# Six or eight column tiles side by side in a decoder layer's first products, in place of four

## The chip, the cores and the metric

The kernel runs on one core of one Trainium2 chip. The metric is the device time of one execution in microseconds; the number given is the median of several executions. All times below are microseconds unless marked ns.

## The reference

One step of a decoder layer on 264 tokens (256 of a prompt, 8 single-token samples), model width 2048:

```
h += 1/2 * RMSNorm_post(SwiGLU_1(RMSNorm_pre(h)))       feed-forward 1, inner width 5632
u  = RMSNorm_pre(h); proj = u @ w_in                    2048 -> 10288 columns:
     conv group (a, b) 2x1024 | z 3072 | xBC 5120 | dt 48
  conv group: GLU -> 31-tap causal convolution -> LayerNorm -> swish
  state-space group: 4-tap causal convolution -> SiLU -> chunked scan
                     (48 heads in 8 groups, state 128) -> RMSNorm gated with SiLU(z)
h += RMSNorm_post(concat(conv 1024, ssm 3072) @ w_out)
h += 1/2 * RMSNorm_post(SwiGLU_2(RMSNorm_pre(h)))       feed-forward 2
h += RMSNorm_post(sigmoid(RMSNorm_pre(h) @ w_gate) * (p @ w_proj))   per-layer embedding
```

Everything is float32, and the states and the sample rows of the convolutions are outputs too.

## The kernel before, in words

Activations lie transposed: features on the 128 partitions, the 264 tokens along a row. A matrix of K rows and M columns is cut into 128x128 weight tiles, K/128 row tiles by M/128 column tiles. The product for one column tile is accumulated in one PSUM bank over all row tiles.

**Three products for one.** A float32 product is made of float32r parts. The input tile is split into a rounded part and the rest (`split`, L248 to L257: ACT rounds, DVE subtracts); so is the weight tile (L151: ACT rounds `whi`; L152: DVE subtracts and leaves `wlo`). `mm3` (L242) issues three matmuls for each pair of tiles, at L244, L245 and L246.

**The weights' stream.** `Weights` (L125) walks a list of units, `_plan` (L70), each at most 16 weight tiles. A unit is loaded in halves of up to 8 tiles (512 KB) by SP, each half rounded by ACT and subtracted by DVE. There are four buffers of 8 tiles for the raw, the rounded and the rest part; two units are asked for ahead of the one in use (`AHEAD`). A buffer comes free when the matmuls that read its tiles are done.

**Two loops over the weights.** `gemm_one` (L342) makes one column tile from one unit of 16 rows: it needs all 16 input tiles. `gemm_first` (L330) is used where a stage's input tiles are only being made: its units hold 4 rows by 4 column tiles, and four banks are accumulated side by side, so that each new input tile is followed by 4 x 3 matmuls. It is called in feed-forward 1 and 2 (L371), in the input projection (L786), in the output projection (L852) and in the per-layer embedding (L928).

**PSUM.** Eight banks: a pool of five for column tiles (`acc_tile`, L184) and a pool of three for everything else (`ps_tile`, L187): the sums of squares, transposes, the state-space part.

**Who reads the banks.**
- Feed-forward: `mid` (L363) takes a gate bank and an up bank: DVE multiplies the gate by the scale `r` (L365), ACT applies SiLU, DVE multiplies by the up bank (L368). `r` comes from the sum of squares over all input tiles (`sq.total()`, L296) through Ln and Exp on ACT.
- Input projection: the order of the column tiles is fixed in `_in_order` (L43): dt, then for each of eight groups B, C, x, (b and a of the conv group in groups 1, 2, 4 and 6), x, x, z, z, z. So the first ten are dt, B, C, x0, x1, x2, z0, z1, z2, B of group 1. `do_dt` (L548) reads its bank once (L551) and then computes time steps and decays, with a round trip through DRAM (L569 to L576) before ACT's Exp at L577. `do_conv` (L598) reads its bank with two ACT instructions (L600, L601) and three of DVE (L603). A z bank is read by one SiLU (L812).
- Per-layer embedding: the bank is read once, times `r` (L939).

**What sets the order.** Instructions are traced in program order, and a scheduler lays them on the engines at compile time by priority (program order; the weights ahead of the rest) and by its own estimate of when each can run. Each engine then works through its list in that fixed order. ACT functions that need a table (SiLU; Ln and Exp) are held in program order by `table` and `act` (L228 to L240), so that a SiLU traced after `do_dt` runs after `do_dt`'s Exp.

Of the kernel before, what the change touches and what calls it, by code (L numbers as in the profile page):

```python
# [21 lines left out]
NS = 8  # L22
# [15 lines left out]

GLU_IN = (1, 2, 4, 6)


# ---------------------------------------------------------------- layout plan
def _in_order():  # L43
    """Column tiles of the input projection in the order they are computed."""
# [25 lines left out]
def _plan():  # L70
    """Weight units in order of use: (matrix, row tiles, column tiles), row tile slowest."""
# [3 lines left out]
    def ffn(i):  # L75
        gu = f"gu{i}"
        for q in range(4):
            plan.append((gu, k16[4 * q : 4 * q + 4], [0, 1, 2, 3]))
        for lo, hi in FF_CHUNKS:
            for f in range(max(lo, 2), hi):  # L80
                plan.append((gu, k16, [2 * f]))
                plan.append((gu, k16, [2 * f + 1]))
            for m in range(KD):
                plan.append((f"dn{i}", list(range(lo, hi)), [m]))
# [4 lines left out]
    first = [m for _, m in IN_ORDER[:4]]  # L89
    for q in range(4):  # L90
        plan.append(("in", k16[4 * q : 4 * q + 4], first))
    for _, m in IN_ORDER[4:]:
        plan.append(("in", k16, [m]))
# [8 lines left out]
    for q in range(4):  # L102
        plan.append(("pg", k16[4 * q : 4 * q + 4], [0, 1, 2, 3]))
    for m in range(4, KD):
        plan.append(("pg", k16, [m]))
# [5 lines left out]
# columns of the small-parameter block  # L111
# [13 lines left out]
class Weights:  # L125
    """Streams the weight units: load, round to float32r, keep what rounding left."""
# [8 lines left out]
    def load(self, between=()):  # L135
        """The next unit, in halves; runs a function of `between` ahead of each half."""
# [29 lines left out]
def kernel(ctx: ExitStack, tc: tile.TileContext, a: dict):  # L166
# [10 lines left out]
    # ------------------------------------------------------------ helpers  # L177
# [50 lines left out]
    def table(name):  # L228
        """Functions that need a table run in program order, so that tables change only here."""
# [18 lines left out]
    def split(x, gain=None):  # L248
        """float32r halves of x (times a gain per partition)."""
# [9 lines left out]
    class SumSq:  # L259
        """Sum of squares over tiles and partitions, on every partition. The last `direct` tiles  # L260
        go to the tensor engine by themselves."""
# [19 lines left out]
        def add_plain(self, s):  # L281
            """Adds the tile s itself."""
# [16 lines left out]
    def rsqrt(out, x, bias=0.0, scale=1.0):  # L299
        """(scale * x + bias) ** -0.5"""  # L300
# [3 lines left out]
    def rms_scale(p, n):  # L304
        """1 / sqrt(p / n + eps)"""
        r = rtile()
        rsqrt(r, p, eps1, 1.0 / n)
        return r

    # ------------------------------------------------------------ constants  # L310
# [10 lines left out]
    # ------------------------------------------------------------ residual stream  # L321
# [5 lines left out]
    bg = deque()  # work that fills in between the matrix products  # L327

    # ------------------------------------------------------------ feed-forward
    def gemm_first(xs, kts, nunits):  # L330
        accs = [acc_tile() for _ in range(4)]
        n = 0
        total = nunits * 4
        for _ in range(nunits):
            w = ws.next()
            for kk in range(4):
                for m in range(4):
                    mm3(accs[m], w[4 * kk + m], xs[kts[n]], n == 0, n == total - 1)
# [13 lines left out]
    def ffn(xs, sq, done):  # L352
        """xs: split gained input; sq: its sum of squares. Calls done(m, y) on each finished
        column tile y (without the input scale); returns eps * (mean square + eps) of the input."""
# [16 lines left out]
        accs = gemm_first(xs, k16, 4)  # L371
        mid(0, accs[0], accs[1])
        mid(1, accs[2], accs[3])
        ys = [None] * KD
        for c, (lo, hi) in enumerate(FF_CHUNKS):
            for f in range(max(lo, 2), hi):
# [20 lines left out]
    def ffn_scale(p, eq):  # L397
        """1 / 2 / sqrt(mean(y^2) + eps / scale^2): the post-norm of scale * y, halved, where
        eq = eps / scale^2."""
# [13 lines left out]
    # ============================================================ FFN 1  # L413
# [8 lines left out]
    for q in range(4):  # L422
        ws.load([lambda k=4 * q + i: load_x(k) for i in (0, 2)])
# [5 lines left out]
    # sample conv history: sums over the saved rows  # L429
# [33 lines left out]
    # y for the post-norm; h . y and y . y (with the gain) for the next pre-norm  # L463
# [22 lines left out]
    # mean square of h + rs y, from the parts  # L486
# [8 lines left out]
    # per-layer embedding projection: independent of the residual stream  # L495
# [13 lines left out]
    # u = rmsnorm(h + rs y), two tiles behind the update of h  # L509
# [15 lines left out]
    # ============================================================ mixer  # L525
# [3 lines left out]
    # causal triangle: row token s, column token l, l >= s  # L529
# [6 lines left out]
    tm = mp.tile([P, 2, 2, NH], F32, name="tm")          # token-major dt, dt*A per chunk  # L536
    acs = mp.tile([P, 2, NH], F32, name="acs")           # token-major cumulative sums
    dte = mp.tile([P, 2, NH], F32, name="dte")           # decay to the end of the chunk
    cd = mp.tile([P, NH], F32, name="cd")                # decay over chunk 1
    dtp = mp.tile([P, 24, NS], F32, name="dtp")          # sample dt on (head, p)  # L540
    eap = cpool.tile([P, 24, NS], F32, name="eap")       # sample decay on (head, p)
# [543 lines left out]
```

## Time and profile before

| | |
|---|---|
| median of 3 executions | 2482.04 (2472.21 to 2486.53) |
| span of the profiled execution, which is all the profile gives of its time | 2479.2 |
| granted TensorE clock, mean | 0.990 |
| matmuls at L244, L245, L246 | 6320 each |
| weight halves of 512 KB, of 256 KB | 774, 32 |
| wait of ACT's weight rounding (L151) on matmuls to free a buffer | 733.5 |
| input tiles made in feed-forward 1 / input projection / feed-forward 2 / embedding, from about | 7 / 796 / 1566 / 2355 |

How to read the views. The table of windows cuts the span into stretches; for each it gives the length, then for each engine the busy time and in brackets the number of instructions, then the granted clock of TensorE (1.00 is full), the share of the DMA engines and GB/s. A busy TensorE can still be slow: matmuls overlap in their records, so their number in a stretch says more than the busy time. The list of waits says which engine waited at which line for which, with the total, the number of times and the longest. A row of the timeline is start, duration, engine, line, operation, output and inputs, and in square brackets the idle time just before with what ended it.

### The profile page before, as it was taken

How to read it: one execution, taken by the hardware profiler on the slowest of the kernel's cores; microseconds unless marked ns; L12 is line 12 of the kernel's file. 1: busy time of each engine (PE TensorE's matmuls, PEld its weight loads, DVE VectorE, ACT ScalarE, POOL GpSimd, SP SyncE). 2: the span in 40 equal slices, each digit the busy share in tenths (PEclk: the TensorE clock that was granted, in tenths of full speed). 3: DMA queues.
4: the chain of work that ended last, by engine and by line, in shares of the span. 5: the costliest groups of instructions: out<-in, count | busy, mean ns of one | idle time of the engine just before them, and what ended most of it. 6: DMA issues, size and time to landing. Idle time of an engine off the chain costs nothing.

```text
span 2479.2 us, 47214 instructions
## 1 busy us (share of the span) xinstructions
PE 2405.7 (97%) x19432; PEld 2380.9 (96%) x19432; DVE 1593.6 (64%) x2249; ACT 1179.2 (48%) x1761; POOL 348.6 (14%) x329
## 2 busy tenths in 40 slices
PE   8999999999999999999999999899999999999996
PEld 8999999999999889999998999899999999999996
DVE  6554455545557858979898965855545655555585
ACT  6444444433456465555655454544444443344463
POOL 2500000000015212121112011410000000000142
PEclk9999999999999999999999999999999999999998
DMA  7655555555556665666665547467666776675653
GB/s 242 211 181 180 180 179 179 180 180 181 181 167 214 200 199 191 214 208 197 210 212 187 180 162 231 140 232 235 221 211 221 237 236 206 210 239 191 193 171 114
DMA packets 160201, 489.88 MB, mean 198 GB/s; under 512 B 23360, under 2 KB 40304, under 8 KB 159984
## 3 DMA queue, kind: packets, MB, share of 16 engines
q1 hardware_dynamic: 159984, 486.85, 60.9%
q8 instruction: 152, 2.49, 0.4%
q14 instruction: 65, 0.53, 0.1%
HBM read 465.65 MB, written 22.42 MB: 197 GB/s over the span
## 4 chain that ended last, share of the span: by engine, by line
PE 86%; DVE 7%; DMA 2%; ACT 2%; issue 2%; POOL 1%; SPq 0%; DVEq 0%; ACTq 0%; POOLq 0%
PE acc L244 28%; PE acc L246 28%; PE acc L245 28%; DVE wlo L152 2%; DVE y L213 1%; DVE h L210 1%; DVE tmp L213 1%; ACT whi L151 1%; DVE act L213 1%; PE ps L729 1%; PE ps L296 0%; POOL run L210 0%; DMA ab<-d_cs 0%; PE ps L714 0%; DMA wraw<-in_w 0%
## 5 line engine op out<-in xcount | busy, mean ns | idle before, releaser
L244 PE MATMUL acc<-act,whi 128*128 128x264 f32 x6320 | 1801.0, 288 | 16.8 <-ACT whi L151 8.4
L245 PE MATMUL acc<-act,whi 128*128 128x264 f32 x6320 | 1804.2, 286 | 12.5 <-DVE act L213 6.3
L246 PE MATMUL acc<-act,wlo 128*128 128x264 f32 x6320 | 1802.4, 286 | 3.6 <-DVE wlo L152 3.6
L152 DVE TENSOR_TENSOR wlo<-wraw,whi 128x1024 fp32r<-128x1024 f32 (+1 forms) x806 | 992.3, 1233 | 612.7 <-ACT whi L151 610.0
L151 ACT CAST whi<-wraw 128x1024 fp32r<-128x1024 f32 (+1 forms) x806 | 828.1, 1031 | 994.7 <-PE acc L245 733.5
L245 PEld LDWEIGHTS acc<-act,whi 128*128 128x128 f32 x6320 | 1203.6, 190 | 17.9 <-DVE act L213 8.6
L246 PEld LDWEIGHTS acc<-act,wlo 128*128 128x128 f32 x6320 | 1199.1, 190 | 7.7 <-DVE wlo L152 5.2
L244 PEld LDWEIGHTS acc<-act,whi 128*128 128x128 f32 x6320 | 1186.6, 189 | 19.9 <-ACT whi L151 8.4
L210 POOL TENSOR_TENSOR run<-run,tmp 128x264 f32<-128x264 f32 x135 | 129.8, 962 | 982.3 <-ACT tmp L237 978.8
L210 POOL TENSOR_TENSOR s<-s,eap 128x1024 f32<-128x1024 f32 x24 | 47.3, 1972 | 608.2 <-DMA s<-in_hst 586.4
L213 DVE SCALAR_TENSOR_TENSOR y<-v,vec,y 128x247 f32<-128x247 f32 (+23 forms) x240 | 124.5, 540 | 1.1
L213 DVE SCALAR_TENSOR_TENSOR s<-bb,xds,s 128x128 f32<-128x128 f32 x192 | 52.6, 347 | 62.9 <-POOL s L210 62.9
L210 POOL TENSOR_TENSOR h<-h,cbc 128x1024 f32<-128x1024 f32 x24 | 65.4, 2738 | 165.3 <-DVE y L213 72.1
L210 DVE TENSOR_TENSOR tmp<-acc,rr 128x264 f32<-128x264 f32 x104 | 44.7, 431 | 64.0 <-PE acc L246 63.9
L252 ACT CAST act<-tmp 128x264 fp32r<-128x264 f32 x120 | 48.6, 409 | 62.3 <-DVE tmp L210 47.5
L210 DVE TENSOR_TENSOR tmp<-tmp,acc 128x264 f32<-128x264 f32 x88 | 37.6, 427 | 45.6 <-PE acc L246 44.8
L210 DVE TENSOR_TENSOR act<-tmp,act 128x264 fp32r<-128x264 f32 x120 | 54.3, 457 | 0.0
L210 DVE TENSOR_TENSOR y<-y,acc 128x264 f32<-128x264 f32 x80 | 34.0, 425 | 26.5 <-PE acc L246 26.5
L237 ACT ACTIVATE tmp<-tmp 128x264 f32<-128x264 f32 x112 | 46.8, 418 | 8.3 <-DVE tmp L210 8.0
L237 ACT ACTIVATE tmp<-y 128x264 f32<-128x264 f32 x67 | 28.1, 426 | 42.3 <-DVE y L210 41.2
L213 DVE SCALAR_TENSOR_TENSOR act<-h,vec,act 128x264 fp32r<-128x264 f32 x48 | 35.2, 756 | 6.4 <-ACT act L237 6.4
L237 ACT ACTIVATE act<-h,vec 128x264 fp32r<-128x264 f32 x48 | 23.8, 512 | 31.3 <-POOL h L210 15.2
(148 smaller groups left out, 800.7 us busy)
## 6 DMA issues: line engine op xcount, KB each, us to landing
wraw<-in_w SPq DMA_DIRECT2D x774, 512.0 KB, 4.7
h<-in_hst SPq DMA_DIRECT2D x24, 512.0 KB, 4.9
s<-in_hst SPq DMA_DIRECT2D x24, 512.0 KB, 6.4
out_nss<-s SPq DMA_DIRECT2D x24, 512.0 KB, 2.8
wraw<-in_w SPq DMA_DIRECT2D x32, 256.0 KB, 3.7
ab<-d_cs SPq DMA_DIRECT2D x16, 384.0 KB, 4.2
cbc<-d_bc SPq DMA_DIRECT2D x8, 512.0 KB, 4.2
bb<-d_bc SPq DMA_DIRECT2D x8, 512.0 KB, 7.4
```

The source lines that it names most:

```text
L151: nc.scalar.copy(hi, raw)
L152: nc.vector.tensor_tensor(out=lo, in0=raw, in1=hi.bitcast(F32), op=ALU.subtract)
L210: return (eng or nc.vector).tensor_tensor(out=out, in0=in0, in1=in1, op=op)
L213: return nc.vector.scalar_tensor_tensor(out=out, in0=in0, scalar=scalar, in1=in1, op0=op0, op1=op1)
L237: i = nc.scalar.activation(out=out, in_=in_, func=func, bias=bias, scale=scale)
L244: nc.tensor.matmul(acc, hi, x[:, 0, :], start=first, stop=False)
L245: nc.tensor.matmul(acc, hi, x[:, 1, :], start=False, stop=False)
L246: nc.tensor.matmul(acc, lo, x[:, 0, :], start=False, stop=last)
L252: nc.scalar.copy(t[:, 0, :], x)
L729: nc.tensor.matmul(pd[64 * q : 64 * q + 64, P * c : P * c + P], xdt[c][:, 2 * j + q, :], ab[c][:, 2 * j + q, :], start=True, stop=True,)
```

## The change

`gemm_first` gets the number of columns as an argument. In feed-forward 1 and 2 and in the per-layer embedding it is 6, in the input projection 8; in the output projection it stays 4. Banks beyond five come from the pool of three: one with 6 columns, three with 8. They are the first ones: the first gate tile, the first embedding tile, and dt, B and C. Units for these calls hold 2 rows by 6 or 8 columns (12 tiles, loaded as 8 and 4; or 16), eight units instead of four. The columns that move into the wide group leave the list of single columns. The loads of feed-forward 1's first units are written out in eight steps of two input tiles and one unit, where they were four steps of two input tiles, half a unit, two input tiles, half a unit. All arithmetic and all weight bytes are the same.

```diff
+FIRST_FF, FIRST_IN, FIRST_PG = 6, 8, 6
...
     def ffn(i):
         gu = f"gu{i}"
-        for q in range(4):
-            plan.append((gu, k16[4 * q : 4 * q + 4], [0, 1, 2, 3]))
+        for q in range(8):
+            plan.append((gu, k16[2 * q : 2 * q + 2], list(range(FIRST_FF))))
         for lo, hi in FF_CHUNKS:
-            for f in range(max(lo, 2), hi):
+            for f in range(max(lo, FIRST_FF // 2), hi):
...
-    first = [m for _, m in IN_ORDER[:4]]
-    for q in range(4):
-        plan.append(("in", k16[4 * q : 4 * q + 4], first))
-    for _, m in IN_ORDER[4:]:
+    first = [m for _, m in IN_ORDER[:FIRST_IN]]
+    for q in range(8):
+        plan.append(("in", k16[2 * q : 2 * q + 2], first))
+    for _, m in IN_ORDER[FIRST_IN:]:
...
-    for q in range(4):
-        plan.append(("pg", k16[4 * q : 4 * q + 4], [0, 1, 2, 3]))
-    for m in range(4, KD):
+    for q in range(8):
+        plan.append(("pg", k16[2 * q : 2 * q + 2], list(range(FIRST_PG))))
+    for m in range(FIRST_PG, KD):
...
-    def gemm_first(xs, kts, nunits):
-        accs = [acc_tile() for _ in range(4)]
+    def gemm_first(xs, kts, nunits, nm=4):
+        accs = [ps_tile([P, T]) if m < nm - 5 else acc_tile() for m in range(nm)]
         n = 0
-        total = nunits * 4
+        per = len(kts) // nunits
         for _ in range(nunits):
             w = ws.next()
-            for kk in range(4):
-                for m in range(4):
-                    mm3(accs[m], w[4 * kk + m], xs[kts[n]], n == 0, n == total - 1)
+            for kk in range(per):
+                for m in range(nm):
+                    mm3(accs[m], w[nm * kk + m], xs[kts[n]], n == 0, n == len(kts) - 1)
                 n += 1
...
-        accs = gemm_first(xs, k16, 4)
-        mid(0, accs[0], accs[1])
-        mid(1, accs[2], accs[3])
+        accs = gemm_first(xs, k16, 8, FIRST_FF)
+        for f in range(FIRST_FF // 2):
+            mid(f, accs[2 * f], accs[2 * f + 1])
...
-    for q in range(4):
-        ws.load([lambda k=4 * q + i: load_x(k) for i in (0, 2)])
+    for q in range(8):
+        ws.load([lambda k=2 * q: load_x(k)])
...
-    first = gemm_first(us, k16, 4)
+    first = gemm_first(us, k16, 8, FIRST_IN)
...
-        acc = first[n] if n < 4 else gemm_one(us, k16)
+        acc = first[n] if n < FIRST_IN else gemm_one(us, k16)
...
-    accs = gemm_first(xs, k16, 4)
+    accs = gemm_first(xs, k16, 8, FIRST_PG)
...
-        acc = accs[m] if m < 4 else gemm_one(xs, k16)
+        acc = accs[m] if m < FIRST_PG else gemm_one(xs, k16)
```

More of the change, by code (lines that the diff above doesn't have):

```diff
@@ L369, in mid @@
             mids[f] = split(p)
-        accs = gemm_first(xs, k16, 4)
-        mid(0, accs[0], accs[1])
-        mid(1, accs[2], accs[3])
+        accs = gemm_first(xs, k16, 8, FIRST_FF)
+        for f in range(FIRST_FF // 2):
+            mid(f, accs[2 * f], accs[2 * f + 1])
         ys = [None] * KD
         for c, (lo, hi) in enumerate(FF_CHUNKS):
-            for f in range(max(lo, 2), hi):
+            for f in range(max(lo, FIRST_FF // 2), hi):
                 pg = gemm_one(xs, k16)
```

## The prediction, made before the changed kernel was run

> **What bounds the kernel now.** I read the page's busy times first, then the table of windows over the stages that call `gemm_first`, then TensorE's waits in those stages, then the timeline at their ends.
>
> ```profile
> span 2479.2 us, 47214 instructions
> PE 2405.7 (97%) x19432; PEld 2380.9 (96%) x19432; DVE 1593.6 (64%) x2249; ACT 1179.2 (48%) x1761; POOL 348.6 (14%) x329
> 310.00:372.00 62.00, 62.00 (x510) 62.00 (x509) 31.80 (x37) 25.33 (x32) 0.00 (x0) 1.00 0.56 179
> ```
>
> TensorE bounds the kernel as a whole. The third row is an undisturbed stretch of feed-forward 1: 510 matmuls in 62 us, 0.1216 us each at the full clock. One column tile of 16 rows is 48 matmuls, 5.83 us; one input tile against four columns is 12 (1.46), against six 18 (2.19), against eight 24 (2.92). The number of these matmuls does not change, so only lost TensorE time can be won.
>
> ```profile
> 802.60:838.60 36.00, 29.43 (x205) 28.06 (x204) 33.38 (x47) 15.64 (x27) 17.45 (x19) 0.91 0.71 235
> 838.60:872.50 33.90, 33.90 (x275) 33.27 (x274) 22.07 (x39) 15.35 (x28) 0.00 (x0) 1.00 0.55 150
> 1568.20:1605.00 36.80, 33.53 (x240) 32.34 (x241) 35.10 (x47) 22.31 (x44) 20.61 (x21) 0.92 0.34 106
> 2357.00:2394.00 37.00, 33.76 (x243) 32.58 (x244) 34.85 (x48) 22.67 (x44) 21.31 (x21) 0.93 0.44 140
> ...
> PE acc L246 <- DVE wlo L152: 1.1, 1, 1.1
> PE ps L296 <- POOL run L210: 0.5, 1, 0.5
> ...
> PE acc L245 <- DVE act L210: 6.0, 4, 1.9
> PE acc L244 <- ACT act L252: 0.5, 1, 0.5
> ...
> PE acc L245 <- DVE act L213: 3.1, 4, 1.1
> ```
>
> Columns of the windows: PE, PEld, DVE, ACT, POOL, clock, DMA. The first row is the input projection's first columns, the third feed-forward 2's, the fourth the embedding's. DVE works 33.4 of 36.0, 35.1 of 36.8 and 34.9 of 37.0: it makes the input tiles and the weights' rest parts, and TensorE waits for it. The waits are those inside the stages: feed-forward 1 (two rows, 1.6 in all), input projection (6.0 + 0.5), feed-forward 2 (3.1; the embedding's answer has the same row). In the input projection 205 matmuls take 24.9 at the full clock, so 11.1 of 36.0 is lost: 6.5 waited, 3.2 to the clock (36.0 x 0.09), the rest to slower pairs. So the change can win at most 1.6 + 11.1 + 3.1 + 3.1 = 18.9, 0.8% of the span.
>
> **The change part by part.** *Balance per input tile.* What DVE spends on weights, and on all else, in the time that the tiles are made:
>
> ```profile
> 1566.40:1602.00 35.60, 19.74 (x70) 14.31 (x70) 10.75 (x8) 0.90 0.33 106
> 802.60:833.00 30.40, 14.93 (x52) 11.35 (x52) 10.71 (x7) 0.89 0.72 238
> L152 DVE TENSOR_TENSOR wlo<-wraw,whi 128x512 fp32r<-128x512 f32 x32 | 22.1, 690 | 0.6
> ```
>
> The first two rows count only instructions that touch `wlo` (third bracket: DVE). Seven subtractions of 8 tiles (the eighth of the first row only begins there) take 10.7, 0.19 per weight tile; the rest of the stretch, 24.9 and 19.7, makes 16 input tiles, 1.55 and 1.23 each. Feed-forward 2: four columns cost DVE 1.55 + 0.76 = 2.31 per tile against TensorE's 1.46; six cost 2.70 against 2.19. DVE stays the slower one, but buffers filled ahead cover some of it. Input projection: 1.23 + 0.76 = 1.99 against 1.46; with eight 2.75 against 2.92. There TensorE becomes the bound, which is why this term is the largest. The units of 12 need a subtraction of 4 tiles each, 690 ns: 0.17 per tile, so the cut costs DVE nothing; twelve more SP issues, casts and subtractions in all are hidden behind DVE's own list.
>
> *The new wait.* With four columns one of the five banks is free when the group ends, so the next column starts at once. With six or eight the pool of five is full: the next `gemm_one` waits until DVE has read a bank, and behind its first matmul on TensorE's list stand all later ones. ACT and DVE are not held and refill two units of weights meanwhile. Also, the waits inside the group can no longer be filled with the next column's matmuls.
>
> ```profile
> 1600.59 1.39 DVE L213 SCALAR_TENSOR_TENSOR act<-h,vec,act 128x264 fp32r<-128x264 f32 x2
> 1605.39 0.43 DVE L210 TENSOR_TENSOR tmp<-tmp,acc 128x264 f32<-128x264 f32 x1 [0.88 <-ACT tmp L237]
> 2389.24 1.40 DVE L213 SCALAR_TENSOR_TENSOR act<-h,vec,act 128x264 fp32r<-128x264 f32 x2
> 2392.68 0.77 DVE L210 TENSOR_TENSOR tmp<-acc,rr 128x264 f32<-128x264 f32 x2 [0.92 <-PE acc L246]
> 1568.26 1.25 PE L244 MATMUL acc<-act,whi 128*128 128x264 f32 x4 [2.94 <-ACT act L237]
> 2357.02 1.25 PE L244 MATMUL acc<-act,whi 128*128 128x264 f32 x4 [3.41 <-ACT act L237]
> ```
>
> *Feed-forward 2.* The last input tile is done at 1602.0. Two units of 12 are ready beforehand, so 72 weight tiles remain, 13.7, and the last tile moves to 1566.4 + 24.9 + 13.7 = 1605.0; TensorE ends 2.19 later, 1607.2. It has then had 1607.2 - 1568.3 = 38.9 for 288 matmuls, 35.0, and 2.9 of half clock (36.8 x 0.08): 1.0 of waits is left, so 2.1 of 3.1 is won. The first bank of the five (the up tile of pair 0) now comes free 3.8 after the last input tile (1602.0 to 1605.8: total, Ln, Exp, gate times `r`, SiLU, times up): 1608.8, a wait of 1.6. Net -0.5.
>
> *Embedding.* The same, but bank two is read only once, 2.8 after the last tile (2390.6 to 2393.4). Wait 2.8 - 2.2 = 0.6; won 2.1 less that, net -1.5.
>
> *Feed-forward 1.* Here TensorE sets the pace already and `r` is known long before the end. Two rows now bring 768 KB of weights and 270 KB of x, and at the rate of this row
>
> ```profile
> 12.00:16.00 4.00, 4.00 (x28) 4.00 (x28) 4.00 (x5) 4.00 (x9) 3.60 (x3) 1.00 1.05 398
> ...
> L237 ACT ACTIVATE tmp<-tmp 128x264 f32<-128x264 f32 x112 | 46.8, 418 | 8.3 <-DVE tmp L210 8.0
> ...
> L152 DVE TENSOR_TENSOR wlo<-wraw,whi 128x1024 fp32r<-128x1024 f32 x774 | 970.2, 1256 | 612.1 <-ACT whi L151 610.0 <-PE acc L246 0.8
> ```
>
> they take 2.7 against 4.4 of matmuls, so x behind the larger weights on SP's list is not late. The 1.6 goes. At the end a gate, SiLU, up chain of 0.43 + 0.42 + 0.43 starts 5 x 0.36 = 1.8 before the group's end: from 0 to one weight subtraction (1.26) late; taken 0.6. Net -1.0.
>
> *Input projection.* A start remains in which the first tiles are late:
>
> ```profile
> 803.40 0.75 PE L244 MATMUL acc<-act,whi 128*128 128x264 f32 x4 [0.51 <-ACT act L252]
> 805.49 0.39 PE L245 MATMUL acc<-act,whi 128*128 128x264 f32 x1 [1.33 <-DVE act L210]
> 838.65 0.48 ACT L237 ACTIVATE h<-acc,vec 48x264 f32<-48x264 f32 x1 [0.89 <-PE acc L246]
> 847.38 0.46 DVE L213 SCALAR_TENSOR_TENSOR h<-acc,vec,h 128x253 f32<-128x253 f32 x1
> 876.41 0.44 PE L688 MATMUL ps<-ident,h 128*128 128x128 f32 x2 [3.39 <-ACT h L237]
> ...
> 876.00:880.00 4.00, 3.59 (x21) 3.59 (x22) 1.42 (x3) 3.93 (x9) 0.00 (x0) 0.69 0.82 233
> ```
>
> 0.51 stays; of 1.33 eight matmuls instead of four cover 0.49, leaving 0.84; of the clock's 3.2 I keep half, 1.6: 3.0 lost at the start. The group ends at about 803.4 + 46.7 + 2.5 = 852.6. The bank that is waited for is x0's, fourth in the order, after B and C on DVE. From below: three convolutions are nine DVE reads of 0.46, 4.2, begun 1.4 before the end, +2.8. From above: x0 was last read at 847.8, 8.1 after its group ended (839.7, three columns after dt), and x0 now ends 1.5 before the group: +6.6. Nothing waited for it then, but the weights' subtractions stood in between as they will now: 5.0, nearer the upper. A gap like that brings a slower clock: the slice behind the 3.39 gap has 0.69, 4 x 0.31 = 1.2. Net -11.1 + 3.0 + 5.0 + 1.2 = -1.9.
>
> In the Trainium skill's page "TensorE: Matmul & The Clock Gate", section "Why this matters for your kernels", an idle gap under about 3 us costs no clock. Two slices of the start speak against taking that as a limit:
>
> ```profile
> 804.00:808.00 4.00, 2.67 (x14) 2.51 (x13) 4.00 (x8) 3.13 (x6) 3.06 (x4) 0.73 0.98 359
> 812.00:816.00 4.00, 3.89 (x19) 3.89 (x20) 4.00 (x6) 0.41 (x1) 3.42 (x4) 0.58 0.88 315
> ...
> 812.11 0.39 PE L245 MATMUL acc<-act,whi 128*128 128x264 f32 x1 [1.91 <-DVE act L210]
> ```
>
> Gaps of no more than 1.33 and 1.91 came with clocks of 0.73 and 0.58. By the page's rule the start would keep its clock and the sum would be 1.6 lower; the row decides, and I keep the 1.6.
>
> *Sum.* -1.0 - 1.9 - 0.5 - 1.5 = -4.9, span 2474.3. The median of the runs is 2.8 above the profiled span: 2477.1.
>
> **The rivals.** *A: the list comes out well.* The scheduler puts the reads of the first banks ahead of the weights, and ACT's weight casts ahead of the Exp that waits for a DRAM round trip:
>
> ```profile
> 873.38 0.36 ACT L237 ACTIVATE eap<-eap 128x192 f32<-128x192 f32 x1 [6.26 <-DMA eap<-d_dt]
> 896.79 0.16 ACT L600 COPY xo<-acc 128x11 f32<-128x11 f32 x1
> 896.85 0.39 ACT L237 ACTIVATE h<-acc 128x264 f32<-128x264 f32 x1
> ```
>
> That Exp blocks ACT for 6.26 now and is followed by the 3.39 gap and its 1.2 of clock. Then: feed-forward 1 -1.6, input projection -11.1 + 3.0 + 2.8 = -5.3, feed-forward 2 -2.1, embedding -2.1, the gap -4.6; -15.7, time 2466.3. For it: the gap is an accident of the order. Against it: a wider first group does not touch the round trip.
>
> *B: the gain is handed back in the mixer.* DVE is the busiest engine behind TensorE there:
>
> ```profile
> 1364.00:1426.00 62.00, 62.00 (x505) 62.00 (x504) 61.14 (x119) 28.56 (x44) 2.70 (x3) 0.99 0.57 180
> ```
>
> 61.1 of 62, with the same work to do. TensorE then runs ahead only to wait later; the input projection is worth 0 and the rest -3.0: 2479.0. Against it: in that very stretch TensorE did not wait.
>
> *C: slower; the dt chain sets the mixer.* dt is read at 838.65 now; it would come at 852.6 - 2.5 = 850.1, 11.4 later, and z0's SiLU, 58.2 after it (896.85), at 908.3, with z0 and z1 holding two of five banks from the group's end. TensorE resumes at 852.6 + 6.2 = 858.8, and z2 and group 1's B, C, x, b, a fill 35.0 plus about 11 of the state-space part and its gaps (eight columns after dt, up to x of group 1, took 58 and not 46.7: its bank is read at 896.8): 904.8; then no bank is left. It decides if the SiLU comes after that point: here by 3.5, and 1.2 of clock. If every later group keeps its distance to dt, the mixer ends 11.4 + 4.7 later, the rest gains 3.0: 2482.0 + 13.1 = 2495.1. Against it: 838.6 to 872.5 ran without a gap, so the chain had slack there.
>
> **How the numbers follow.** A measurement of this kernel can tell about 0.5%, 12.4 us, from no change. Forecast 0.41, A 0.26, B 0.22, C 0.11. A alone is faster by more than that; C alone slower; forecast and B lie within: 0.26, 0.63, 0.11. The range runs from A, less the 4 that runs scatter, to where half of C is left out: 2462 to 2491.
>
> **What would show it.** Right: in the windows of the four stages the waits of L245 for DVE's input tiles fall to about 1 each, and TensorE shows a new wait at L244 right behind each group, 1.6 in feed-forward 2, 0.6 in the embedding, about 5 in the input projection, released by DVE's bank reads; DVE's `wlo` work inside the stages grows by a third to two thirds. Wrong: no wait behind the group of eight (A); 3 us or more lost later in the mixer at z's SiLU or at the state-space matmuls (B, C); or waits inside the groups as long as before, which would mean that the weights, not the input tiles, are late.

## The result, and the profile after

The changed kernel takes 2505.72 us (median of 4 executions, 2504.94 to 2509.49) beside 2479.74 for the kernel before on the same chip (4, 2472.21 to 2486.53; three of these gave the 2482.04 ahead of the prediction): a ratio of 1.0111, 95% interval 1.0089 to 1.0134. It is slower by 1.1%. The forecast was 2477.1 with a range to 2491; slower by over 0.5% had a chance of 0.11. Of the profiled execution (2504.94) the span is 2503.2, 24.0 more than before's.

In the changed file the lines lie three further down up to about L580 (`mm3` is L247, L248, L249; ACT's weight rounding L154, DVE's subtraction L155, the sum's matmul L299) and four behind it.

Each stage ends in the sum of squares over its result, whose first matmul reads POOL's running sum. These matmuls cut the span into stages; the last one ends with the span. The second, from the input projection to the end of the output projection, is called the mixer below. TensorE's timeline, first the changed kernel, then the kernel before:

```profile
793.05 0.61 PE L299 MATMUL ps<-run,ones 128*128 128x264 f32 x2
...
1564.41 0.61 PE L299 MATMUL ps<-run,ones 128*128 128x264 f32 x2
...
2364.62 0.61 PE L299 MATMUL ps<-run,ones 128*128 128x264 f32 x2
```

```profile
789.27 0.61 PE L296 MATMUL ps<-run,ones 128*128 128x264 f32 x2
...
1562.72 0.61 PE L296 MATMUL ps<-run,ones 128*128 128x264 f32 x2
...
2351.01 0.61 PE L296 MATMUL ps<-run,ones 128*128 128x264 f32 x2
```

| | feed-forward 1 | projection and mixer | feed-forward 2 | embedding | span |
|---|---|---|---|---|---|
| before | 789.27 | 773.45 | 788.29 | 128.19 | 2479.2 |
| changed | 793.05 | 771.36 | 800.21 | 138.58 | 2503.2 |
| difference | +3.8 | -2.1 | +11.9 | +10.4 | +24.0 |
| forecast | -1.0 | -1.9 | -0.5 | -1.5 | -4.9 |

So the loss lies in the three stages with six columns, and there in two waits of TensorE. Its waits over the whole run, changed and before (total, number, longest):

```profile
PE ps L299 <- POOL run L213: 26.9, 10, 8.4
PE acc L247 <- ACT whi L154: 18.1, 5, 7.8
...
PE acc L247 <- DVE h L216: 6.3, 1, 6.3
PE ps L692 <- ACT h L240: 5.1, 1, 5.1
...
PE ps L249 <- DVE wlo L155: 1.7, 3, 0.7
...
PE ps L248 <- DVE act L213: 1.4, 2, 1.0
```

```profile
PE ps L296 <- POOL run L210: 12.8, 8, 2.8
PE acc L244 <- ACT whi L151: 8.4, 1, 8.4
...
PE acc L245 <- DVE act L213: 6.3, 8, 1.1
PE acc L245 <- DVE act L210: 6.0, 4, 1.9
```

The first two waits, for POOL's running sum and for ACT's rounding of weights, have grown by 14.1 and 9.7 (8.4 and 7.8 of the second are the kernel's first weights); the waits for DVE's input tiles have fallen from 6.3 and 6.0 to 1.4. Feed-forward 2 shows how. TensorE's timeline of the changed kernel, ACT's, and the windows of that stretch:

```profile
1587.95 0.39 PE L247 MATMUL acc<-act,whi 128*128 128x264 f32 x1 [3.03 <-ACT whi L154]
...
1599.11 1.25 PE L299 MATMUL ps<-run,ones 128*128 128x264 f32 x2 [7.31 <-POOL run L213]
1599.78 0.80 PE L247 MATMUL ps<-act,whi 128*128 128x264 f32 x1
```

```profile
1586.87 1.03 ACT L154 CAST whi<-wraw 128x1024 fp32r<-128x1024 f32 x1
...
1601.49 0.62 ACT L154 CAST whi<-wraw 128x512 fp32r<-128x512 f32 x1 [2.47 <-PE ps L248]
```

```profile
1569.90:1588.00 18.10, 14.00 (x91) 13.37 (x91) 16.35 (x27) 9.78 (x22) 11.22 (x12) 0.86 0.13 45
1588.00:1599.10 11.10, 3.80 (x18) 3.49 (x18) 10.04 (x14) 5.08 (x13) 8.35 (x9) 0.68 0.15 48
1599.10:1622.00 22.90, 22.89 (x173) 22.62 (x174) 11.38 (x14) 11.29 (x15) 0.00 (x0) 0.93 0.57 182
```

The output's name tells the bank: `acc` is the pool of five, `ps` the pool of three. Column 0 has a `ps` bank, and its first matmul in the stage stands at 1599.78, right behind the sum of squares, which can only run when the last input tile is there. In the 11.1 us before it TensorE does 18 matmuls, and in the 22.9 behind it 173. Between the casts at 1586.87 and 1601.49 ACT rounds no weights, and what lets it go on is a matmul on `ps`: the four weight buffers hold tiles that column 0 has not read yet. The embedding has the same picture (a wait of 8.36 for the running sum at 2399.05).

### The profile page after: what moved, and what is told of

The parts are those of the page before. It is cut to its first block, busy times and chain, and to the rows that moved or that the text cites. A ratio compares the mean times of both kernels' runs of the same rounds, so it can differ in the third digit from the quotient of the medians.

```text
span 2503.2 us, 47290 instructions
## 1 busy us (share of the span) xinstructions
PE 2407.1 (96%) x19432; PEld 2381.5 (95%) x19432; DVE 1595.8 (64%) x2261; ACT 1182.5 (47%) x1773; POOL 343.5 (14%) x329
## 5 line engine op out<-in xcount | busy, mean ns | idle before, releaser
L247 PE MATMUL acc<-act,whi 128*128 128x264 f32 x6224 | 1787.3, 288 | 33.4 <-ACT whi L154 18.1
L249 PE MATMUL acc<-act,wlo 128*128 128x264 f32 x6224 | 1771.3, 286 | 3.4 <-DVE wlo L155 3.4
L248 PE MATMUL acc<-act,whi 128*128 128x264 f32 x6224 | 1774.5, 285 | 0.0
L155 DVE TENSOR_TENSOR wlo<-wraw,whi 128x1024 fp32r<-128x1024 f32 (+1 forms) x818 | 999.1, 1224 | 644.4 <-ACT whi L154 639.4
L154 ACT CAST whi<-wraw 128x1024 fp32r<-128x1024 f32 (+1 forms) x818 | 830.6, 1019 | 1021.6 <-PE acc L248 736.8
L247 PEld LDWEIGHTS acc<-act,whi 128*128 128x128 f32 x6224 | 1173.6, 189 | 37.6 <-ACT whi L154 18.9
L248 PEld LDWEIGHTS acc<-act,whi 128*128 128x128 f32 x6224 | 1183.2, 190 | 1.5 <-issue 0.4
L249 PEld LDWEIGHTS acc<-act,wlo 128*128 128x128 f32 x6224 | 1176.6, 190 | 7.1 <-DVE wlo L155 4.8
L213 POOL TENSOR_TENSOR run<-run,tmp 128x264 f32<-128x264 f32 x135 | 124.6, 923 | 996.9 <-ACT tmp L240 965.7
L213 DVE TENSOR_TENSOR tmp<-acc,rr 128x264 f32<-128x264 f32 x101 | 43.5, 431 | 63.3 <-PE acc L249 63.3
L299 PE MATMUL ps<-run,ones 128*128 128x264 f32 x38 | 14.8, 476 | 27.0 <-POOL run L213 26.9
```

The source lines that it names most:

```text
L154: nc.scalar.copy(hi, raw)
L155: nc.vector.tensor_tensor(out=lo, in0=raw, in1=hi.bitcast(F32), op=ALU.subtract)
L213: return (eng or nc.vector).tensor_tensor(out=out, in0=in0, in1=in1, op=op)
L247: nc.tensor.matmul(acc, hi, x[:, 0, :], start=first, stop=False)
L248: nc.tensor.matmul(acc, hi, x[:, 1, :], start=False, stop=False)
L249: nc.tensor.matmul(acc, lo, x[:, 0, :], start=False, stop=last)
```

## The experiments

Theory (bank): the pool of three gives its banks in the order in which the program asks. The sum of squares is asked for ahead of the group, so column 0 stands behind it on TensorE's list; the other columns run on for two units and then lack weights. Rival (width and units): six columns from units of twelve starve TensorE in any case. Each ratio is taken against executions of the kernel before on the same chip, and can differ a little from the quotient of the two medians. The stage times are read like those above, from one execution each.

| run | median | ratio, 95% interval | ff 1 | mixer | ff 2 | emb. |
|---|---|---|---|---|---|---|
| before | | | 789.27 | 773.45 | 788.29 | 128.19 |
| changed | 2505.72 | 1.0111 [1.0089, 1.0134] | 793.05 | 771.36 | 800.21 | 138.58 |
| e1 bank alone | 2509.61 | 1.0111 [1.0091, 1.0132] | 794.21 | 774.84 | 798.82 | 140.93 |
| e2 own place | 2493.10 | 1.0047 [1.0031, 1.0063] | 790.99 | 785.97 | 787.82 | 126.82 |
| e3 eight alone | 2477.55 | 0.9986 [0.9975, 0.9996] | 788.83 | 770.21 | 788.04 | 128.72 |
| e4 units alone | 2480.19 | 0.9999 [0.9987, 1.0011] | 788.64 | 774.23 | 787.50 | 128.23 |
| e5 own place by stage | 2482.21 | 1.0011 [1.0001, 1.0021] | 791.55 | 776.33 | 787.68 | 127.54 |
| e6 sum after | 2489.01 | 1.0044 [1.0030, 1.0058] | 791.36 | 772.66 | 790.22 | 131.96 |
| e7 six in projection | 2484.61 | 1.0021 [1.0010, 1.0032] | 788.67 | 779.72 | 785.78 | 128.43 |
| e8 eight, embedding five | 2481.01 | 1.0009 [0.9997, 1.0020] | 789.83 | 776.97 | 787.79 | 129.01 |
| e9 eight, banks changed | 2496.22 | 1.0055 [1.0040, 1.0071] | 788.65 | 791.70 | 787.89 | 128.26 |
| e10 late stages alone | 2479.59 | 0.9995 [0.9984, 1.0006] | 788.36 | 776.42 | 787.97 | 126.95 |
| e11 e9 and e10 | 2493.27 | 1.0054 [1.0038, 1.0070] | 788.73 | 787.38 | 788.51 | 126.98 |
| e12 Exp first, four | 2482.92 | 1.0011 [1.0002, 1.0019] | 788.95 | 774.21 | 787.53 | 128.51 |
| e13 Exp first, eight | 2479.39 | 1.0004 [0.9992, 1.0015] | 789.59 | 771.20 | 788.04 | 128.67 |
| e14 Exp first, e9 | 2495.84 | 1.0064 [1.0051, 1.0076] | 789.21 | 784.15 | 787.52 | 127.92 |
| e15 Exp first, e11 | 2494.03 | 1.0064 [1.0050, 1.0079] | 789.42 | 794.88 | 788.44 | 126.96 |
| e16 full units | 2479.46 | 0.9993 [0.9977, 1.0008] | 791.49 | 774.16 | 791.39 | 126.86 |

**e1: the bank alone.** The kernel before with one edit, in the three stages that have six columns in the change:

```diff
-    def gemm_first(xs, kts, nunits):
-        accs = [acc_tile() for _ in range(4)]
+    def gemm_first(xs, kts, nunits, nps=0):
+        accs = [ps_tile([P, T]) if m < nps else acc_tile() for m in range(4)]
...
```

with `nps` 1 in both feed-forwards and the embedding, 0 elsewhere.

> Four columns and units of four rows everywhere, as before; only column 0 of the first group of both feed-forwards and of the embedding takes its bank from the pool of the sums (ps) and no longer from the pool of five. Bank theory: that pool gives its banks in program order, and the sum of squares was asked for first, so column 0 stands on TensorE's list behind the sum, which waits for the last input tile; its weights stay in the buffers, so after two units no weights come, and 118 of the 192 matmuls (14 us) are left when the sum is done. Loss of 10 to 13 in feed-forward 2 and in the embedding, 3 to 7 in feed-forward 1, none in the input projection: about 2508, 1.1% over before; TensorE waits 6 to 9 us once in each stage for POOL's running sum, ahead of the sum's matmuls. Rival, width and units: neither has changed, so before's time, 2480 within 5.

2509.61, and +4.9, +10.5 and +12.7 in the three stages, +1.4 in the mixer. TensorE in feed-forward 2:

```profile
1600.30 1.25 PE L296 MATMUL ps<-run,ones 128*128 128x264 f32 x2 [12.38 <-POOL run L210]
1600.97 0.80 PE L244 MATMUL ps<-act,whi 128*128 128x264 f32 x1
```

The loss is there without a single wider group or smaller unit. Only the wait ahead of the sum was expected shorter, 6 to 9: it is 12.4 in the two late stages, and 3.35 in feed-forward 1.

**e4: the units alone.** `FIRST_FF, FIRST_IN, FIRST_PG = 4, 4, 4` in the changed kernel: four columns, units of two rows.

> Four columns everywhere, as before, but all first groups from units of two rows (eight weight tiles) in place of four rows (sixteen), so one step of weights per unit and half as many tiles ahead. Bank theory: the cut of the units is no cause, so within 3 to 8 of before, 2480 to 2488, all from fewer tiles held ahead of the group. Rival, units: the smaller units are what makes weights late in the change, so a loss of 10 or more: 2490 to 2506.

No difference: units of two rows are not the cause. (With four columns such a unit is one full half of 8 tiles.)

**e2 and e5: a place of its own for column 0.** The change with six, eight and six columns, and the pool of three cut into three places of one bank, taken in turn. In e2 everywhere:

```diff
-    ps = ctx.enter_context(tc.tile_pool(name="ps", bufs=3, space=PS))
+    ps = ctx.enter_context(tc.tile_pool(name="ps", bufs=1, space=PS))
...
+    turn = [0]
...
-        return ps.tile(shape, F32, tag="ps", bufs=3, name=nm("ps"))
+        turn[0] += 1
+        return ps.tile(shape, F32, tag=f"ps{turn[0] % 3}", bufs=1, name=nm("ps"))
```

In e5 the pool is closed and opened anew ahead of the input projection (one place of three banks) and ahead of feed-forward 2 (three places again).

> 6, 8 and 6 columns and their units as in the change; only the three banks of the pool of sums become three places of one bank each, taken in turn, so that column 0 and the sum of squares no longer share one. Bank theory: column 0 runs from the group's start, the losses of 6.2, 11.9 and 10.4 in feed-forward 1, feed-forward 2 and the embedding vanish, and the gains forecast for them may show: 2472 to 2480. Rival, width and units: units of twelve and the full pool of accumulators cost the time, so it stays at 2500 to 2506.

> 6, 8 and 6 columns; the three banks of sums are three places of one bank in the feed-forwards and the embedding, so that column 0 does not stand behind the sum, and one pool of three in the mixer, as in the change. Bank theory, with the stages that the runs so far showed (first feed-forward +1.7, mixer -2.1 to -3.2, second -0.5, embedding -1.4, each against before): span 2476, so 2475 to 2479. Rival: the fixed turn is not what cost the mixer 12.5 us in the run with three places everywhere, but the wide groups around it: 2490 or more.

In both, feed-forward 2 and the embedding are back at or under before's times. e2's feed-forward 2, with column 0 at the start and a short wait at the sum:

```profile
1582.48 0.41 PE L250 MATMUL ps<-act,whi 128*128 128x264 f32 x1 [2.93 <-ACT act L243]
...
1615.90 0.71 PE L302 MATMUL ps<-run,ones 128*128 128x264 f32 x2 [1.07 <-POOL run L216]
```

e2's total missed its range, since with the fixed turn the mixer takes 12.5 longer (785.97); one wait of 7.15 there, again for a running sum, is most of what can be named. With one pool in the mixer (e5) it is 776.33, and the rival of e5 falls. e5 itself came 3 above its range's end.

**e6: the sum asked for last.** `p = sq.total()`, `r` and `eq` are traced behind `gemm_first`; in the embedding likewise.

> The change, but the sum of squares asks for its bank behind the first group in the program (both feed-forwards and the embedding), so that column 0 comes first in the pool's order and the sum last. Bank theory: TensorE no longer waits for the running sum in the middle of the group, but the input scale comes only behind the group, and the first bank of the five is read that much later: the sum's pair, Ln, Exp, gate, SiLU and up, 3 to 5 us of wait behind each group in place of 6 to 12 lost: 2484 to 2495. Rival, width and units: 2500 or more, as the change.

As the theory says: no wait in the middle of the groups, but 4.33 behind that of feed-forward 2 and 5.02 behind the embedding's, because `r` now comes late. Two kinds of edit, a place of its own (e2, e5) and a later request for the sum (e6), take the loss in the late stages away, whole or for the most part, and e1 brings it without the width: the bank theory is shown.

**e3: eight columns in the input projection alone.** `FIRST_FF, FIRST_IN, FIRST_PG = 4, 8, 4`.

> Eight columns in the input projection alone; the feed-forwards and the embedding as before. Bank theory: the sums of the stage before are done when the input projection starts, its three extra banks are free, and the stage keeps what the change's trace shows for the mixer, 4.5 us: 2475, 0.2% under before. The prediction's terms for this stage: 1.9 under before, 2478. Rival, width and units: a wide group costs here too, 2480 or more; rival C of the prediction: 2493.

0.9986, the best of all, but not a firm gain: e8 has the same lists on every engine up to the embedding, and reads 776.97 in the mixer where e3 reads 770.21. Its ratio, taken on another chip, is 1.0009, outside e3's interval, so differences of some 0.2% say little here.

**e8: five columns in the embedding.** `4, 8, 5`: all banks from the pool of five.

> Eight columns in the input projection, four in the feed-forwards, five in the embedding, which needs no bank of the sums: column 0 is free from the start without any other edit. Bank theory: the embedding gains 0.5 to 1.5 against four columns, where six lost 10.4: 2474 to 2477. Rival, width: a full pool of five costs the embedding 3 or more: 2480 or more.

1.0009, above the expectation, but not as the rival has it: the embedding is 129.01, neither the gain of the theory nor a loss of 3. The 4 us above the range are less than the mixer differs by between e3 and e8.

**e7: six columns in the input projection.** `4, 6, 4`.

> Six columns in the input projection (units of twelve), four everywhere else. The group now ends with x1 or z0 and the first bank of the five that is asked for again is B's, first in DVE's and ACT's order and not behind two convolutions. Theory, that the wait of 6.3 us behind the group of eight is the queue of convolutions ahead of x0's bank: the wait falls to 2 to 4, the waits inside the group grow by 1 to 2, and the time is 2475 to 2478, no worse than eight columns. Rival, that the wait is the work that must follow dt in any case (the dt chain): the stage's end does not move with the width, and the time is that of four columns, 2480.

The wait behind the group falls to 4.14 only, and waits of 4.25 and 3.30 follow at the first state-space part; mixer 779.72. With 2484.61 neither the theory nor its rival has the time: what follows the group matters as much as the wait.

**e9: other columns in the banks.** Eight columns; x0, x1, x2 take the banks of the pool of three, and dt, B, C, z0, z1 the five.

```diff
-    def gemm_first(xs, kts, nunits, nm=4):
+    def gemm_first(xs, kts, nunits, nm=4, side=()):
...
-        accs = [ps_tile([P, T]) if m < nm - 5 else acc_tile() for m in range(nm)]
+        accs = [ps_tile([P, T]) if m in (side or range(nm - 5)) else acc_tile() for m in range(nm)]
...
-    first = gemm_first(us, k16, 8, FIRST_IN)
+    first = gemm_first(us, k16, 8, FIRST_IN, (3, 4, 5))
```

> Eight columns in the input projection, four elsewhere, as in the run with eight there alone; only which columns take the banks of the pool of sums is changed: x0, x1 and x2 take them, and dt, B, C, z0 and z1 take the five. Theory, that the wait of 6.26 us behind the group is the first of the five banks, x0's, being read last among five convolutions that DVE runs in turn: the next column now asks for dt's bank, which ACT reads once and at once, so the wait falls to 1 or less, and TensorE keeps the lead of 47 matmuls (5.7 us) that it has over before's at 60 us into the stage: 2470 to 2474 if it lasts. Rival B of the prediction, the mixer hands it back: no such wait, but the time stays at 2477 to 2480, with the lead gone by the second group's state-space part.

The wait behind the group is gone, as forecast, and the kernel is 0.55% slower. Windows from the stage's start, before, changed, e9:

```profile
789.27:849.27 60.00, 53.43 (x392) 51.66 (x391) 54.26 (x83) 33.58 (x70) 24.30 (x26) 0.94 0.71 234
849.27:869.27 20.00, 20.00 (x162) 19.37 (x161) 12.06 (x18) 7.73 (x11) 0.00 (x0) 1.00 0.60 165
```

```profile
793.05:853.05 60.00, 56.35 (x440) 54.41 (x438) 51.89 (x69) 32.16 (x59) 25.68 (x26) 1.00 0.78 259
853.05:873.05 20.00, 13.74 (x99) 13.18 (x98) 14.86 (x31) 8.50 (x20) 0.00 (x0) 0.83 0.33 111
```

```profile
788.65:848.65 60.00, 56.40 (x441) 54.60 (x440) 51.92 (x68) 32.22 (x59) 25.50 (x26) 1.00 0.76 258
848.65:888.65 40.00, 37.50 (x303) 36.62 (x302) 25.80 (x47) 17.44 (x36) 0.00 (x0) 1.00 0.54 152
888.65:908.65 20.00, 4.70 (x14) 2.87 (x14) 7.15 (x12) 14.07 (x30) 0.00 (x0) 0.54 0.46 132
```

At 60 us the group of eight is 48 matmuls (5.8 us) ahead of before's. At 80 it is 15 behind (392 + 162 in before, 440 + 99 in the changed kernel). e9 does not lose there, and then, from 100 us on, stands almost still: 14 matmuls in 20 us at a granted clock of 0.54. TensorE's and ACT's rows in that stretch:

```profile
891.37 0.69 PE L692 MATMUL ps<-ident,h 128*128 128x128 f32 x2 [5.22 <-ACT h L240]
903.85 0.90 PE L692 MATMUL ps<-ident,h 128*128 128x128 f32 x3 [10.94 <-ACT h L240]
```

```profile
887.77 0.36 ACT L240 ACTIVATE eap<-eap 128x192 f32<-128x192 f32 x1 [8.04 <-DMA eap<-d_dt]
...
895.63 0.99 ACT L240 ACTIVATE ab<-ab,acs 128x128 f32<-128x128 f32 x3 [1.96 <-DMA ab<-d_cs]
```

The transposes of the first state-space part wait for x's SiLUs on ACT, and those stand behind steps of the dt chain (what `do_dt` computes from dt's bank), two of which wait for transfers through DRAM, `d_dt` and `d_cs`. The chain itself is late, and DVE's rows show where. Its last step ahead of the transfers, in the changed kernel and in e9:

```profile
869.28 0.35 DVE L570 TENSOR_SCALAR h<-h,na 48x264 f32<-48x264 f32 x1
```

```profile
871.93 0.35 DVE L570 TENSOR_SCALAR h<-h,na 48x264 f32<-48x264 f32 x1
```

And the stretch from the chain's first step on DVE (L558) to that one, counting only instructions that touch `wlo` (third bracket: DVE), in the same two runs:

```profile
863.90:869.30 5.40, 2.48 (x7) 1.99 (x7) 0.00 (x0) 0.59 0.31 97
```

```profile
859.30:872.00 12.70, 9.78 (x35) 6.51 (x35) 6.10 (x5) 1.00 0.63 206
```

ACT reads dt's bank at the same place, 63.8 and 63.6 into the stage, but L570 comes at 76.2 and at 83.3. While TensorE stands in its wait of 6.26, few weight buffers come free (ACT's rounding waits 4.8 for one there), and DVE runs the chain without a subtraction in between; in e9 five of them, 6.1 us, stand among its steps. So e9's rival holds in its mechanism, the mixer hands the lead back, but it had the time at 2477 to 2480, and the run is 16 over that.

**e10 and e11: what is left, put together.** e10 has four columns in feed-forward 1 and the projection, six with a place of its own in the two late stages; e11 adds e9's group.

> Four columns in the first feed-forward and in the input projection; six in the second feed-forward and in the embedding, with a bank of its own for column 0 there. What is left are two terms of the forecast by themselves, -0.5 and -1.5, with the bank free as the forecast took it: 2476 to 2480. Rival, width: +2 or more, 2481 or over.

> Four columns in the first feed-forward; eight in the input projection with x0, x1 and x2 in the banks of the sums; six in the second feed-forward and in the embedding with a bank of its own for column 0. If the parts add up, -6 for the input projection and -1 to -2 for the two late stages: 2470 to 2474, 0.2 to 0.4% under before. If the mixer hands its part back: 2477 to 2480.

e10: 0.9995; the embedding gains 1.2, feed-forward 2 0.3, against the profile of before. e11 carries e9's loss and is outside both of its ranges.

**e12 to e15: ACT's Exp ahead of the round trip.** The Exp of the sample decay is taken on the 48 rows before they go to DRAM:

```diff
-        nc.sync.dma_start(d_dt[1], dta[:, NP_:])
+        dx = mp.tile([P, NS], F32, name="dx")
+        act(dx[:NH], dta[:, NP_:], AF.Exp)
+        nc.sync.dma_start(d_dt[1], dx[:NH])
...
-        act(eap, eap, AF.Exp)
```

in the kernel before (e12), in e3 (e13), e9 (e14) and e11 (e15).

> The kernel before (four columns everywhere) with one edit in the dt chain: the Exp of the sample tokens' decay is taken on 48 partitions ahead of the round trip through DRAM, and not on the copy that comes back, so ACT no longer stands in front of that transfer (6.26 us in the trace of before), with weight casts and the SiLUs of B, C and x behind it. The result is the same. Theory, that ACT's stand at the round trip sets the first state-space part: TensorE's waits of 3.4 and 1.6 at the first transposes shrink, 2475 to 2478. Rival, that the transfer of the decays, d_cs, which comes right behind, sets it just as well: no change, 2480.

> Eight columns in the input projection alone (first three columns in the banks of the sums), with the Exp ahead of the round trip. Theory: the first state-space part no longer waits for the 4 to 9 us stand of ACT at a round trip that starts 7 us later than with four columns; 3 to 6 under the same kernel without the edit, so 2472 to 2476, and the first state-space part 105 to 108 us into the stage in place of 111 to 114. Rival, the wait of 6.3 behind the group is what costs: it stays, and with it 2477 to 2481.

> As the last, with x0, x1 and x2 in the banks of the sums, so that no wait stands behind the group. Theory: without the Exp in ACT's way most of the 16.2 us at the first transposes goes; 8 to 14 under the 2496 of the same banks, 2482 to 2488, or below 2476 if the transposes come free altogether. Rival: the dt chain itself (DVE's and ACT's small steps behind weights that now go on uninterrupted) and the transfer of d_cs are late, and the Exp only stood where they would have: 2490 or more.

> The last, with six columns and a bank of its own for column 0 in the second feed-forward and the embedding: 1 to 2 under it by those two terms. Rival, as for the last.

My theory fell, and the rivals hold: 1.0011, 1.0004, 1.0064, 1.0064. ACT now stands at the next transfer of the same chain, and TensorE's wait at the first transposes is one instead of several. e14, TensorE and ACT:

```profile
902.83 0.90 PE L693 MATMUL ps<-ident,h 128*128 128x128 f32 x3 [15.47 <-ACT h L240]
```

```profile
894.61 0.98 ACT L240 ACTIVATE ab<-ab,acs 128x128 f32<-128x128 f32 x3 [7.81 <-DMA ab<-d_cs]
```

In e12 the same row of ACT waits 5.80. So the Exp was not what held ACT up: the chain from dt through both transfers is late by itself.

**e16: full weight buffers.** e5 with four columns in the projection, and the feed-forwards' first units four rows by six columns (three halves of 8). The loads of feed-forward 1's first units go back to four steps with it.

> Six columns in the feed-forwards and in the embedding with a bank of its own for column 0 there, four in the input projection; the feed-forwards' first units hold four rows by six columns, 24 tiles in three full halves of 8, in place of 12 in halves of 8 and 4. Theory, that the first feed-forward's own loss of 1.7 to 2.3 us with six columns comes from the half of 4 that takes a whole buffer of 8 (24 tiles ahead in place of 32, 8.8 us of matmuls in place of 11.7, while ACT makes twelve input tiles in a row): the wait of 1.9 to 3.4 us for ACT's rounding at 21 us falls to 1 or less and the stage ends at 789 to 790.2. Rival, that six columns ask more of DVE than it can give there: the wait only moves, and the stage ends at 791 or later.

Half right. The waits for ACT's rounding in feed-forward 1, in e2 and in e5,

```profile
20.74 0.39 PE L250 MATMUL ps<-act,whi 128*128 128x264 f32 x1 [1.89 <-ACT whi L154]
```

```profile
21.32 0.59 PE L257 MATMUL ps<-act,whi 128*128 128x264 f32 x1 [3.24 <-ACT whi L154]
```

are gone in e16, as they would be if the half-filled buffers were their cause; e16 also changes the order in which x and the weights are loaded, so it does not show that alone. But a wait behind the group came in their place, larger than the 1.16 of e2 and e5, and the stage ends at 791.49 all the same (feed-forward 2, at 791.39, has two such waits, 2.86 at the sum and 2.62 behind the group):

```profile
49.77 0.59 PE L257 MATMUL acc<-act,whi 128*128 128x264 f32 x1 [2.61 <-DVE tmp L223]
```

## Why the prediction was wrong

**The step that failed.** It is in "The new wait" and the sums for feed-forward 2, the embedding and feed-forward 1. I asked when the pool of five is full behind the group, and took the sixth bank as free at the group's start, at no cost and without a reason. It is asked for behind the sum of squares in the same pool. "72 weight tiles remain ... TensorE ends 2.19 later, 1607.2" held for five columns only; column 0 began at 1599.78, with some 180 of the group's 288 matmuls still to do (288 less the 91 and 18 of the windows). That is +11.9 and +10.4 where -0.5 and -1.5 were forecast. The sign I had named for it, "waits inside the groups as long as before, which would mean that the weights, not the input tiles, are late", did show (3.03 for ACT's rounding, then 7.31 for the sum), but the weights were late there because nobody read column 0's.

**Feed-forward 2 and the embedding with the bank free.** The embedding comes out as forecast. Over e2, e5, e10, e11, e15 and e16 the embedding takes 127.0 on average (126.82 to 127.54), with four columns 128.4 (127.92 to 128.72, eight runs): -1.4, forecast -1.5. Its terms agree less: in e10 1.4 is waited for the weights' rest parts and 1.1 at the sum, nothing behind the group, where 1.0 inside and 0.6 behind it were taken. Feed-forward 2 gains 0.5 in e2 and 0.6 in e5 against the profile of before, but against the nine runs with four columns (mean 787.6) the five with six and units of twelve (788.1) gain nothing; why is open. Its wait behind the group, forecast 1.6, is 1.16 in the changed kernel.

**Feed-forward 1**, forecast -1.0, loses 2.3 with the bank free (791.0 to 791.6 in e2, e5, e6 and e16, mean 791.3, against 789.0 in twelve runs with four columns). The step was "the 1.6 goes": I asked whether x is late on SP's queue, but not whether weights are: a half of 4 tiles uses up a buffer of 8, and TensorE waits 1.89 to 3.38 for ACT's rounding in e2, e5 and e6. In e16 that wait is gone, and the end is still late by a wait behind the group of 2.61, forecast 0.6.

**Input projection.** The sum -1.9 and the stage's -2.1 agree by accident. Its terms: the group ends 65.8 into the stage (865.13 less 6.26, less 793.05) where 63.3 was forecast (852.6 less 789.27), and the wait behind it, from x0's bank as said, is

```profile
865.13 0.56 PE L247 MATMUL acc<-act,whi 128*128 128x264 f32 x1 [6.26 <-DVE h L216]
```

6.26 and not 5.0, near the upper bound of 6.6. DVE takes the convolutions of B, C, x0, x1 and x2 in turn, so the first bank comes free nearly last. The start is off too: from its first matmul (807.38) the group takes 51.5, 4.8 over the 46.7 of its matmuls, where 2.5 was taken. The 1.6 of slower clock in that sum did not come (the granted clock is 1.00 in the first 60 us), but waits of 1.7 for the weights' rest parts did, which the sum had at nothing, beside 1.4 for input tiles. By 80 us the stretch has lost 1.8 (15 matmuls) where 1.9 was to be won. What the mixer's end shows is within the scatter of the rest: with eight columns as in the change 771.36, 770.21, 776.33, 772.66 and 776.97, mean 773.5; with four 774.6 (773.45, 774.84, 774.23, 776.42, 774.16).

**The rivals.** ACT's first read of dt's bank in the changed kernel:

```profile
856.85 0.47 ACT L240 ACTIVATE h<-ps,vec 48x264 f32<-48x264 f32 x1
```

C's mechanism is there: this read comes 63.8 into the stage in place of 49.4 (856.85 less 793.05, 838.65 less 789.27; 14.4 later, forecast 11.4), and the first state update comes 113.6 into it in place of 105.1. Its price was not paid: by the fourth group the two kernels stand level (293.5 and 293.7), as "the chain had slack there" said. e9 and e14 show what it costs when TensorE does arrive early. B is the better name for the projection: what the group wins is handed back within 20 us, to the work that hangs on dt and on its neighbours' convolutions. A needed a gain in all four stages; even with the bank free only the embedding has one clear of the scatter.

**With every bank free** the parts are +2.3, -1.1, +0.5 and -1.4, no change in sum, and e5 measures 1.0011. No version tried beats the kernel before clearly: e3's interval ends at 0.9996, and e8, with the same lists up to the embedding, has 1.0009.

## What to carry to other kernels

Before taking a buffer from another pool, ask who else asks that pool and in which order: a tile that is asked for later stands behind an earlier one, whatever that waits for, and a column that stands still holds every weight buffer it shares with the columns that run. When a wait is removed, look at what was hidden under it: in e9 the 6.3 us behind the group went, and the waits at the first transposes rose from 5.1 to 16.2. And a stage total that agrees with the forecast says nothing until its terms do.

## What the runs showed of the hardware

TensorE's granted clock after a single gap, first in feed-forward 1: a gap of 1.89 (e2, ended at 20.74) leaves it at 1.00, one of 2.61 (e16, ended at 49.77) is followed by 0.50 for 2 us and 0.76 for the next 2. Windows of e2 and of e16:

```profile
20.00:22.00 2.00, 1.26 (x10) 1.26 (x11) 2.00 (x4) 2.00 (x4) 1.84 (x3) 1.00 0.00 0
22.00:24.00 2.00, 1.60 (x8) 0.92 (x6) 2.00 (x4) 1.11 (x3) 0.63 (x1) 1.00 0.03 8
```

```profile
50.00:52.00 2.00, 2.00 (x10) 2.00 (x11) 1.73 (x6) 1.28 (x4) 0.00 (x0) 0.50 0.75 204
52.00:54.00 2.00, 2.00 (x15) 2.00 (x15) 0.75 (x2) 0.41 (x1) 0.00 (x0) 0.76 0.96 336
```

The Trainium skill's page "TensorE: Matmul & The Clock Gate", section "Why this matters for your kernels", asks for no gaps over some 3 us, so that shorter ones go free. For the 1.89 the trace agrees; for the 2.61 it does not. The two do not mark a limit either. In the kernel before a gap of 1.83 is followed by 0.50, and in e1 one of 3.26 leaves the clock at 1.00, neither with another gap of over 0.3 us in the 7 us ahead of it. Rows of before and of e1:

```profile
1067.95 0.71 PE L296 MATMUL ps<-run,ones 128*128 128x264 f32 x2 [1.83 <-POOL run L210]
...
1070.00:1072.00 2.00, 2.00 (x11) 2.00 (x10) 0.97 (x3) 1.99 (x4) 0.00 (x0) 0.50 0.73 254
```

```profile
881.22 0.44 PE L688 MATMUL ps<-ident,h 128*128 128x128 f32 x2 [3.26 <-ACT h L237]
...
882.00:884.00 2.00, 2.00 (x18) 2.00 (x18) 0.44 (x1) 1.99 (x4) 0.00 (x0) 1.00 1.02 294
```

So the length of a gap alone does not tell here whether the clock falls. The slow slices that the prediction held against the page (0.73 and 0.58 beside gaps of 1.33 and 1.91) lie in a stretch of many gaps, so they do not show what a single short gap does; the 1.83 of before does.
